# Up projection of an encoder's MLP as seven block products, with weight sums that grow in one buffer

## The chip, the cores and the metric

One core of one Trainium2 chip runs the whole kernel. The metric is the device time of one execution in microseconds; the time of a kernel is the median of several runs.

## The reference

One encoder layer on 512 tokens of width 1024 in float32: a mixer of two recurrent head groups, cross-attention on 256 memory tokens, and an MLP, each behind an RMSNorm and added to the residual stream, with one more RMSNorm at the end. The change lies in the MLP and in the passage to it.

```python
def squared_relu_mlp(xn, w_up, w_down):
    return jnp.square(jax.nn.relu(xn @ w_up)) @ w_down

x = x + cross_attention(rmsnorm(x, norm_xattn), rmsnorm(mem, norm_mem), w_xq, w_xkv, w_xo)
x = x + squared_relu_mlp(rmsnorm(x, norm_mlp), w_up, w_down)
return rmsnorm(x, norm_final)
```

w_up is 1024 x 4096, w_down 4096 x 1024.

## The kernel before

**Products.** Every float32 operand is split in two parts, hi (a rounded copy, made by ACT) and lo (the rest, made by DVE); `split_out` (L257, L258) issues both. A product takes three matmuls: hi hi, hi lo, lo hi (`mm3`, L261 to L263, and L1153 to L1155 in the block products). Weights arrive in blocks of 128x1024 (512 KB).

**The MLP** goes through the 4096 inner columns in four groups f of 1024. Each f has an up stage, then a down stage. Up is computed with the weights stationary and the 512 tokens as the moving columns: `proj_d` (L274 on) takes 8 blocks of 128 inner columns, each 8 k tiles of `mm3` on 128x512, 192 matmuls for an f. Result blocks leave PSUM through one DVE instruction that applies relu and 1/rms of the token (L1342, the row `rrow` is made by `rms_row`, L1264), and ACT squares them (L1343). DVE and ACT then form sums and differences of token and inner-column halves, and their hi and lo parts (L1349 to L1366), as operands of down.

**Down** and the attention's output projection before it ("xo") already run as seven block products (`by_blocks`, L1135 on): tokens, inner columns and output columns are halved, P1 to P7 are products of sums of token/inner blocks with sums of weight blocks (Winograd's form of Strassen's scheme), and each product is added with a sign to one or two result blocks (`INTO`). Each product comes in two parts g, so that a stage has 14 jobs of 12 matmuls of 128x512 (168 for a down stage). P1, P2 and P3 use plain weight blocks. The sums for P4 to P7 are made by DMA: GpSimd's queue loads a block and then adds others into it with accumulating DMAs (`add_block` L1100, L1102; `sum_loads` L1086). A sum that has been split for one product is added to once more, and serves another (for down, the buffer of P6 becomes that of P4).

**Order.** PE's order is the program's. A job's weights are split up to three jobs ahead (`ahead`), and loaded by SyncE's queue (`load`, L232 on) three blocks ahead of that; `st`, `wh` and `wl` have three buffers each. Weight sums lie in two buffers of 2 x 1024 ("as") and four of 1024 ("gate"). DVE, ACT, GpSimd and SyncE work in the order in which the instructions stand in their queues.

**The passage into up.** The last product of xo is P4. As x (`vv`) is completed block by block, `turn_two` (L1230) transposes 128x128 pieces on PE, eight at a time, and ACT and DVE make hi and lo of x times the norm's gain (L1242, L1243). x is not divided by its rms here. `first_two` (L1305) computes up's first two blocks in halves of k, so that the last x blocks are transposed in between.

Of the kernel before, what the change touches and what calls it, by code (L numbers as in the profile page):

```python
# [45 lines left out]
def _split_order():  # L46
# [30 lines left out]
NSTREAM = len(SEQ) - 10  # L77
# [3 lines left out]
def trunk(ctx: ExitStack, tc: tile.TileContext, x, mem, wpk, vec, cst, lmask, rmask, rows, out):  # L81
# [994 lines left out]
    ORDER = ("P1", "P2", "P6", "P5", "P7", "P3", "P4")  # L1076
    LATE = [(p, g) for p in ORDER[2:] for g in range(2)]
    JOBS = {f: [("P1", 0), ("P2", 0), ("P1", 1), ("P2", 1)] + LATE for f in range(4)}

    JOBS[-1] = [(p, g) for p in ("P1", "P7", "P2", "P5", "P6", "P3", "P4") for g in range(2)]  # L1080
# [5 lines left out]
    def sum_loads(f, names):  # L1086

        parts = {"T2": ((0, 1), (1, 1), (0, 0)), "U": ((0, 1), (0, 0)), "T3": ((0, 1), (1, 1))}
        for nme in names:
            if nme == "T3":  # L1090
                t2 = [G4()[:, :] for _ in range(2)]
            else:
                t = A16()
                t2 = [t[:, g * 1024:g * 1024 + 1024] for g in range(2)]
            for g in range(2):
                sums[f, nme, g] = t2[g]
        return [add_block(sums[f, nme, g], block(f, g, *parts[nme][i]), i > 0)
                for i in range(3) for nme in names for g in range(2) if i < len(parts[nme])]
# [6 lines left out]
    SUMS = {f: {"P6": "T2", "P5": "U", "P7": "T3", "P4": "T2"} for f in range(4)}  # L1105
    SUMS[-1] = {"P6": "T3", "P5": "U", "P7": "T3", "P4": "T3"}

    def job(f, n):

        if n >= len(JOBS[f]):  # L1110
            if f < 3:
                split(SIDX["d", "up", 0, 1024 * (f + 1)] + n - len(JOBS[f]))
            return None
        p, g = JOBS[f][n]
        if p in PLAIN:
            i = block(f, g, *PLAIN[p])
            split(i)
            return hl_tiles[i]
        if (f, n) not in jobs_hl:
            s_ = sums[f, SUMS[f][p], g]  # L1120
            hi, lo = T("wh", 1024, 3, F32R), T("wl", 1024, 3, F32R)
            made = split_out(hi, lo, s_)
            if f < 0 and n == 2:
                for a, b in zip(made, q_made[0]):
                    behind(a, b)
            jobs_hl[f, n] = (hi, lo)
            if f < 0 and p == "P7":
                add_block(s_, block(f, g, 0, 0))
            if p == "P6":
                add_block(s_, block(f, g, 1, 0))  # L1130
        return jobs_hl[f, n]
# [4 lines left out]
    INTO = {f: INTO for f in range(4)}  # L1136
    INTO[-1] = {**INTO[0], "P6": [(2, 1, -1), (0, 1, -1)], "P7": [(2, 1, -1), (2, 0, 1)]}
    LAST = {f: {("P2", 0, 0), ("P3", 0, 1), ("P4", 2, 0), ("P7" if f >= 0 else "P6", 2, 1)} for f in JOBS}

    def by_blocks(f, sta, banks, done, ready=None, after=None):  # L1140

        user = {"P1": 0, "P2": 1, "P5": 2, "P6": 0, "P3": 2, "P7": 0 if f >= 0 else 3, "P4": 0}
        opens = {"P1", "P2", "P5"} if f >= 0 else {"P1", "P2", "P5", "P7"}
# [15 lines left out]
        def ahead(n):  # L1159
            with tc.high_priority():  # L1160
                for m in range(n, n + 3):
                    job(f, m)
# [3 lines left out]
            if n == 8 and 0 <= f < 3:  # L1166
                sum_loads(f + 1, ("U", "T3"))
            return job(f, n)

        def finished(p, u):  # L1170
            for t0, c, sign in INTO[f][p]:
                done(t0 + u, c, held[user[p]][u], sign, (p, t0, c) in LAST[f])

        n = 0
        while n < len(JOBS[f]):
# [287 lines left out]
```

## Time and profile before

| | |
|---|---|
| median of 3 runs | 832.43 us (832.4 to 832.55) |
| profiled execution | 832.41 us, span 830.3 us |
| granted TensorE clock | 0.998 |
| PE, PEld, DVE, ACT busy | 99%, 82%, 72%, 52% of the span |
| GpSimd busy (with its DMA issues) | 77.4 us, 9% |
| DMA moved | 118.86 MB: 77.80 by hardware queue q1 (SyncE's), 39.85 by software queue q0 (GpSimd's) |
| last product of xo begins, up begins | 488.60 us, 494.94 us |

A row of a timeline is: start, duration, engine, line, operation, output <- inputs, shape, and in brackets the idle time of the engine before it and what ended it. PE is TensorE, PEld its weight loads, POOL GpSimd; an "x8" folds eight of the same. A matmul's duration reaches from its issue to the end of its result, so neighbours overlap; distances between starts say what one takes of PE. A row of the DMA queues has packets, MB and the share of the 16 DMA engines' time. A row of the DMA issues has the count, the size and the median time from issue to landing.

### The profile page before, as it was taken

The numbers are of one execution on the slowest core, as the hardware profiler recorded it, in microseconds if no ns is written. First come the engines' busy times: TensorE is split into PE (matmuls) and PEld (weight loads), VectorE is DVE, ScalarE is ACT, GpSimd is POOL, SyncE is SP. The second block draws the span as 40 slices with busy tenths as digits, with TensorE's granted clock in tenths as the row PEclk, the third lists the DMA queues.
The fourth block names the chain that finished last, engine by engine and source line by source line (L and its number), as shares of the span: only waits on it lengthen the run. The fifth ranks groups of instructions, "written<-read, shape, count | busy, mean of one in ns | idle before, by whom it ended". The sixth has DMA issues, their size and how long they took to land.

```text
span 830.3 us, 11722 instructions
## 1 busy us (share of the span) xinstructions
PE 818.2 (99%) x4414; PEld 681.7 (82%) x4414; DVE 594.5 (72%) x1046; ACT 430.0 (52%) x767; POOL 77.4 (9%) x131
## 2 busy tenths in 40 slices
PE   8999999999999999999999999999999999999996
PEld 6788888887878989887888888888888888888885
DVE  6568875699569988555558985676568666756685
ACT  5247455443678475455546575453444345434544
POOL 2000000100010000100000004012102210220001
PEclk9999999999999999999999999999999999999999
DMA  7332223222342344532352349969836982798332
GB/s 276 117 133 78 77 78 102 79 89 79 117 123 68 123 138 147 151 98 85 118 127 60 84 124 299 264 158 270 238 102 176 274 214 98 185 293 206 109 69 102
DMA packets 34122, 118.86 MB, mean 143 GB/s; under 512 B 3921, under 2 KB 4049, under 8 KB 34066
## 3 DMA queue, kind: packets, MB, share of 16 engines
q1 hardware_dynamic: 22832, 77.80, 27.4%
q0 software_dynamic: 10944, 39.85, 21.7%
q8 instruction: 35, 0.57, 0.3%
q10 hardware_dynamic: 290, 0.47, 0.2%
q14 instruction: 21, 0.17, 0.1%
HBM read 116.00 MB, written 2.10 MB: 142 GB/s over the span
## 4 chain that ended last, share of the span: by engine, by line
PE 89%; issue 5%; DVE 2%; DMA 1%; ACT 1%; POOL 1%; POOLq 0%; ACTq 0%
PE mm L261 18%; PE mm L263 18%; PE mm L262 18%; PE sm L1155 6%; PE sm L1153 6%; PE sm L1154 6%; PE sm L485 2%; PE mm L1155 2%; PE mm L1153 2%; PE mm L1154 2%; PE sm L827 1%; PE sm L562 1%; DVE wl L258 1%; PE sm L263 1%; PE sm L261 1%
## 5 line engine op out<-in xcount | busy, mean ns | idle before, releaser
L258 ACT ACTIVATE wh<-st 128x1024 fp32r<-128x1024 f32 x131 | 138.7, 1060 | 189.8 <-PE mm L262 117.8
L261 PE MATMUL mm<-xT,wh 128*128 128x512 f32 x544 | 215.2, 396 | 0.0
L258 DVE TENSOR_TENSOR wl<-st,wh 128x1024 fp32r<-128x1024 f32 x131 | 160.2, 1224 | 75.5 <-ACT wh L258 75.0
L263 PE MATMUL mm<-xT,wl 128*128 128x512 f32 x544 | 213.0, 392 | 0.1
L262 PE MATMUL mm<-xT,wh 128*128 128x512 f32 x544 | 212.3, 390 | 0.3 <-DVE xT L975 0.3
L263 PEld LDWEIGHTS mm<-xT,wl 128*128 128x128 f32 x544 | 102.1, 188 | 21.7 <-DVE wl L258 0.3
L262 PEld LDWEIGHTS mm<-xT,wh 128*128 128x128 f32 x544 | 102.2, 188 | 21.0 <-DVE xT L975 0.9
L261 PEld LDWEIGHTS mm<-xT,wh 128*128 128x128 f32 x544 | 102.2, 188 | 20.9 <-ACT wh L258 0.3
L1102 POOL DMA_DIRECT2D as<-in_wpk x52 | 39.6, 764 | 250.2 <-DVE wl L258 165.1
L1342 DVE SCALAR_TENSOR_TENSOR t<-mm,rg 128x512 f32<-128x512 f32 x32 | 22.0, 691 | 52.1 <-PE mm L263 52.0
L1153 PE MATMUL sm<-wh,yT 128*128 128x512 f32 x128 | 49.8, 389 | 0.0
L1154 PE MATMUL sm<-wl,yT 128*128 128x512 f32 x128 | 49.8, 389 | 0.0
L1155 PE MATMUL sm<-wh,yT 128*128 128x512 f32 x128 | 49.8, 389 | 0.0
L258 ACT ACTIVATE wh<-as 128x1024 fp32r<-128x1024 f32 x26 | 27.6, 1062 | 37.0 <-PE sm L1155 23.7
L258 DVE TENSOR_TENSOR wl<-as,wh 128x1024 fp32r<-128x1024 f32 x26 | 31.9, 1226 | 14.0 <-ACT wh L258 13.9
L1153 PE MATMUL sm<-wh,a 128*128 128x512 f32 x84 | 32.9, 391 | 0.0
L1155 PE MATMUL sm<-wh,a 128*128 128x512 f32 x84 | 32.7, 389 | 0.0
L1154 PE MATMUL sm<-wl,a 128*128 128x512 f32 x84 | 32.7, 389 | 0.0
L1285 DVE TENSOR_TENSOR vv<-vv,sm 128x512 f32<-128x512 f32 x48 | 31.0, 681 | 1.7 <-PE sm L1155 1.7
L199 POOL TENSOR_TENSOR tiny<-tiny,misc 128x4 f32<-128x4 f32 (+1 forms) x10 | 9.6, 963 | 204.6 <-DVE tiny L197 139.5
L1154 PEld LDWEIGHTS sm<-wl,yT 128*128 128x128 f32 x128 | 24.0, 188 | 5.0
L1155 PEld LDWEIGHTS sm<-wh,yT 128*128 128x128 f32 x128 | 24.0, 188 | 5.0
(329 smaller groups left out, 1581.1 us busy)
## 6 DMA issues: line engine op xcount, KB each, us to landing
st<-in_wpk SPq DMA_DIRECT2D x131, 512.0 KB, 3.4
as<-in_wpk POOLq DMA_DIRECT2D x52, 512.0 KB, 7.0
gate<-in_wpk POOLq DMA_DIRECT2D x24, 512.0 KB, 6.9
as<-in_x SPq DMA_DIRECT2D x4, 512.0 KB, 6.7
vv<-in_x SPq DMA_DIRECT2D x8, 256.0 KB, 4.5
out<-vv SPq DMA_DIRECT2D x7, 256.0 KB, 2.2
a<-in_mem SPq DMA_DIRECT2D x2, 512.0 KB, 3.7
t<-in_rows SPq DMA_DIRECT2D x2, 256.0 KB, 4.9
```

The lines of the kernel that those rows point to most:

```text
L199: gp.tensor_tensor(out=r, in0=ms, in1=nh.to_broadcast([P, w]), op=ALU.pow)
L258: return sc.activation(dst_hi, src, AF.Copy), v.tensor_tensor(out=dst_lo, in0=src, in1=dst_hi.bitcast(F32), op=ALU.subtract)
L261: pe.matmul(ps, lhsT=ah, rhs=bh, start=first, stop=False)
L262: pe.matmul(ps, lhsT=ah, rhs=bl, start=False, stop=False)
L263: pe.matmul(ps, lhsT=al, rhs=bh, start=False, stop=last)
L485: mm = pe.matmul(ps[64 * i:64 * i + 64, z:z + 64], lhsT=kc[j][:, w * P + 64 * i:w * P + 64 * i + 64], rhs=rhs(j, w * P, i), start=True, st ...
L1102: return gp.dma_start(out=dst, in_=wpk[idx], **kw)
L1153: pe.matmul(ps, lhsT=ah, rhs=bh, start=new, stop=False, **fl)
L1154: pe.matmul(ps, lhsT=ah, rhs=bl, start=False, stop=False, **fl)
L1155: pe.matmul(ps, lhsT=al, rhs=bh, start=False, stop=end and k == 1, **fl)
L1285: added = v.tensor_tensor(out=z, in0=z, in1=ps, op=ALU.add if sign > 0 else ALU.subtract)
L1342: v.scalar_tensor_tensor(out=y, in0=ps, scalar=0.0, in1=rrow[:, 0:512], op0=ALU.max, op1=ALU.mult)
```

## The change

Up becomes seven block products too, and up and down share one list of jobs for the MLP's eight stages (st = 0 to 7; even ones are up).

- Up: an f has 14 jobs (`MORDER`) of 24 matmuls of 128x256 (256 tokens), 336 for an f (L1468 to L1470). Its blocks are halves of tokens, of inner columns and of the 1024 inputs. Results stay in PSUM over several products (bank A of P1 grows by P6, P7 and P4) and are copied or added from there by ACT and DVE; relu and square are two ACT instructions.
- x is multiplied by 1/rms before the products. `rstd_half` gets 1/rms for each token half (GpSimd's power, L1348), `norm_half` spreads it over rows (two transposes and an ACT copy), `times_r` (L1355) multiplies x blocks of 128x512, and DVE and ACT form the seven operands and their hi and lo parts once, for all four f. `flip` does the transposes; `later` and `after_product` put them between matmuls.
- Weight sums, up and down alike: the P5 sum is split, added to for P6, split, added to for P4, all in one buffer (`chain_buf`); P7 has another (`pair_buf`). The two "as" buffers swap these parts from stage to stage. The "gate" buffers no longer hold weight sums in the MLP. A stage has 8 accumulating and 4 plain DMAs on GpSimd's queue and 6 plain ones on SyncE's. Before, an up and a down stage together had 10 accumulating and 6 plain on GpSimd's and 14 on SyncE's. Up's blocks are read from DRAM in rows of 2 KB (`128x2x512`).
- The order of products in down is now P1, P2, P5, P3, P6, P7, P4 (P6, P5, P7, P3, P4 behind P1 and P2 before). Up's first sums are issued from job 8 of xo on.

```diff
-        for j in range(4):
-            seq += d("up", 1024 * f + P * j, 1) + d("up", 1024 * f + P * (j + 4), 1)
+        for g in range(2):
+            seq += d("up", 1024 * f + 256 * g, 2) + d("up", 1024 * f + 512 + 256 * g, 2)
...
+    MORDER = [("P1", 0), ("P2", 0), ("P1", 1), ("P2", 1)] + [(p, g) for p in ("P5", "P3", "P6", "P7", "P4") for g in range(2)]
+    MJ = [(st, p, g) for st in range(8) for p, g in MORDER]
...
+    def mblock(st, g, kh, c):
+        f = st // 2
+        if st % 2:
+            return wpk[block(f, g, kh, c)]
+        i = SIDX["d", "up", 0, 1024 * f + 512 * c + 256 * g]
+        return wpk[i:i + 2, :, kh * 512:kh * 512 + 512].rearrange("n p c -> p n c")
...
+    def chain_buf(st, g):
+        return msum[st % 2][:, g * 1024:g * 1024 + 1024]
+
+    def pair_buf(st, g):
+        return chain_buf(st + 1, g)
+
+    def sum_start(st, pair):
+        if st < 8:
+            for i, b in enumerate(((0, 1), (1, 1) if pair else (0, 0))):
+                for g in range(2):
+                    mfill(gp, (pair_buf if pair else chain_buf)(st, g), st, g, b, i > 0)
...
+    def msplit(n):
...
+            src = mst[n][:, :] if p in PLAIN else (pair_buf if p == "P7" else chain_buf)(st, g)
+            hi, lo = T("wh", 1024, 3, F32R), T("wl", 1024, 3, F32R)
+            split_out(hi, lo, src)
...
+            if p == "P5":
+                adds.append(mfill(gp, src, st, g, (1, 1), True))
+            if p == "P6":
+                mfill(gp, src, st, g, (1, 0), True)
+            if g == 1 and p in ("P7", "P4"):
+                sum_start(st + 1, p == "P4")
...
+    def mahead(n):
+        with tc.high_priority():
+            for m in range(n, n + 3):
+                msplit(m)
+            for m in range(n + 3, n + 7):
+                mload(m)
+        return mhl[n]
...
+            if n == 8:
+                msum.extend([A16(), A16()])
+                sum_start(0, False)
+                sum_start(0, True)
...
     def add_out(t, c, ps, sign, last):
...
+        if (t, c) == (2, 0):
+            turn_x2[0] = [smb(), smb()]
+            later.append([1, lambda: flip(turn_x2[0], (2,), 0)])
+        elif (t, c) == (3, 0):
+            later.append([0, lambda: flip(turn_x2[0], (3,), 0)])
+            later.append([1, lambda: norm_half(1)])
...
+    def times_r(x, u, h):
+        z = x[:, h * 512:h * 512 + 512]
+        r = rrow[:, u * 256:u * 256 + 256]
+        v.tensor_tensor(out=z.rearrange("p (k t) -> p k t", t=256), in0=z.rearrange("p (k t) -> p k t", t=256),
+                        in1=r.unsqueeze(1).to_broadcast([P, 2, 256]), op=ALU.mult)
...
+    def norm_half(u):
+        ps = smb()
+        for t in range(2):
+            pe.transpose(ps[:, t * P:t * P + P], rt[u][:, t:t + 1].to_broadcast([P, P]), ident)
+        with tc.high_priority():
+            sc.activation(rrow[:, u * 256:u * 256 + 256], ps[:, 0:256], AF.Copy)
+            for p, x in ((("P1", fx[0, 0]), ("P2", fx[0, 1])) if u == 0 else (("P5", sraw[0]),)):
+                for h in range(2):
+                    times_r(x, u, h)
+                    part_split(p, x, h)
...
+    def up(st):
...
+        for n, (p, g) in enumerate(MORDER):
+            hi, lo = mahead(len(MORDER) * st + n)
...
+            ps = B[g] if p == "P2" else C[g] if p in ("P5", "P3") else A[g]
+            xh, xl = xf[p]
+            for k in range(2):
+                o = ps[:, k * 256:k * 256 + 256]
+                for kt in range(4):
+                    z = slice(k * 512 + kt * P, k * 512 + kt * P + P)
+                    m = slice(kt * 256, kt * 256 + 256)
+                    new = k == kt == 0 and p in ("P1", "P2", "P5")
+                    pe.matmul(o, lhsT=hi[:, z], rhs=xh[:, m], start=new, stop=False, **fl)
+                    pe.matmul(o, lhsT=hi[:, z], rhs=xl[:, m], start=False, stop=False, **fl)
+                    pe.matmul(o, lhsT=lo[:, z], rhs=xh[:, m], start=False, stop=kt == 3, **fl)
+                after_product()
...
     for f in range(4):
...
-                y = T2()[:, 0:512]
-                v.scalar_tensor_tensor(out=y, in0=ps, scalar=0.0, in1=rrow[:, 0:512], op0=ALU.max, op1=ALU.mult)
-                sc.activation(y, y, AF.Square)
...
+        sta = up(2 * f)
...
+        by_blocks(2 * f + 1, sta, (sm2, mm2, mm2), lambda t, c, ps, sign, last: add_to(t, c, ps, sign, f == 3 and last))
```

Two places in the order. The first is DVE at the end of xo. `vv_530` and `vv_531` are the last two blocks of x that P4 completes; `xT` are operands of up, `wl` lo parts of weights, `a4` x blocks, `rg` the row of 1/rms. Before, from one of these additions to the other:

```order
L1222 TENSOR_TENSOR vv_530_3315<-vv_530_3315,mm_694_4302 128x512
L1243 SCALAR_TENSOR_TENSOR xT_693_4299<-sm_767_4705,vc_68,xT_693_4299 128x256 x2
L1243 SCALAR_TENSOR_TENSOR xT_693_4299<-sm_768_4714,vc_68,xT_693_4299 128x256
L258 TENSOR_TENSOR wl_765_4688<-st_745_4567,wh_764_4687 128x1024
L1243 SCALAR_TENSOR_TENSOR xT_693_4299<-sm_768_4714,vc_68,xT_693_4299 128x256
L1222 TENSOR_TENSOR vv_531_3317<-vv_531_3317,mm_695_4303 128x512
```

After:

```order
L1299 TENSOR_TENSOR vv_530_3315<-vv_530_3315,mm_701_4309 128x512
L1355 TENSOR_TENSOR a4_751_4577<-a4_751_4577,rg_700_4308 128x512 x2
L1355 TENSOR_TENSOR a4_782_4724<-a4_782_4724,rg_700_4308 128x512
L258 TENSOR_TENSOR xT_692_4298<-a4_751_4577,xT_692_4298 128x512
L258 TENSOR_TENSOR wl_779_4705<-st_759_4615,wh_778_4704 128x1024
L258 TENSOR_TENSOR wl_792_4782<-st_764_4641,wh_791_4781 128x1024
L258 TENSOR_TENSOR xT_692_4298<-a4_751_4577,xT_692_4298 128x512
L258 TENSOR_TENSOR xT_692_4298<-a4_782_4724,xT_692_4298 128x512
L1355 TENSOR_TENSOR a4_782_4724<-a4_782_4724,rg_700_4308 128x512
L1299 TENSOR_TENSOR vv_531_3317<-vv_531_3317,mm_702_4310 128x512
```

Four transposed parts of x (L1243) and one weight split stood between the two additions; now four multiplications by 1/rms, three splits of up's operands and two weight splits do.

The second is GpSimd's queue there. `gate` are the weight sums of xo (the rows of gate_630 and gate_631 at L1096 are L1102 before), `as` the buffers of the MLP's sums, the row that makes `tiny` from `tiny` and `misc` is the power for 1/rms. Before:

```order
L1102 DMA gate_630_3958<-in_wpk 128x1024 [waits DMASW1_49,DVE_49]
L1102 DMA gate_631_3959<-in_wpk 128x1024 [waits DMASW3_49,DVE_49]
L1102 DMA gate_630_3958<-in_wpk 128x1024 [waits DMASW0_49,DVE_49]
L1102 DMA gate_631_3959<-in_wpk 128x1024 [waits DMASW1_49,DVE_49]
L1261 TENSOR_TENSOR tiny_773_4745<-tiny_772_4743,misc_73 128x4 [waits DVE_49,Pool_49]
L1102 DMA as_775_4748<-in_wpk 128x1024 [waits DMAHW7_49,DMAHW6_49,PE_49]
L1102 DMA as_775_4748<-in_wpk 128x1024
L1102 DMA as_776_4749<-in_wpk 128x1024 [waits DMASW7_49,DMASW6_49]
L1102 DMA as_776_4749<-in_wpk 128x1024
```

After:

```order
L1141 DMA as_755_4589<-in_wpk 128x2x512 [waits DMAHW6_49,DMAHW7_49,DVE_49,PE_49]
L1141 DMA as_755_4589<-in_wpk 128x2x512
L1141 DMA as_755_4589<-in_wpk 128x2x512 [waits DMASW2_49]
L1141 DMA as_755_4589<-in_wpk 128x2x512 [waits DMASW3_49]
L1141 DMA as_756_4590<-in_wpk 128x2x512 [waits DMASW7_49,DMASW6_49,DVE_49]
L1096 DMA gate_630_3958<-in_wpk 128x1024 [waits DMASW0_49,DVE_49]
L1141 DMA as_756_4590<-in_wpk 128x2x512
L1141 DMA as_756_4590<-in_wpk 128x2x512 [waits DMASW6_49,DMASW1_49]
L1096 DMA gate_631_3959<-in_wpk 128x1024 [waits DVE_49]
L1141 DMA as_756_4590<-in_wpk 128x2x512 [waits DMASW0_49]
```

The last additions to gate_630 and gate_631 stood alone, ahead of the power and of the MLP's sums; now transfers of up's sums stand before them, between them and behind them, all eight ahead of the power.

More of the change, by code (lines that the diff above doesn't have):

```diff
@@ L1218, in heads_in, with after_product @@
             drain()
+    later = []
+    def after_product():
+        for w in list(later):
+            w[0] -= 1
+            if w[0] < 0:
+                later.remove(w)
+                w[1]()
+    fx, rt, sraw = {}, {}, [None]
     def add_out(t, c, ps, sign, last):
         z = xr[t, c]
[L1222 to L1223 removed]
+        v.tensor_tensor(out=z, in0=z, in1=ps, op=ALU.add if sign > 0 else ALU.subtract)
+        if not last:
+            return
+        with (tc.high_priority() if (t, c) in ((1, 1), (3, 0)) else ExitStack()):
```

317 lines of the change are left out of this document (176 added, 141 removed).

## The prediction

> **What bounds the kernel now.** I read the page first: the busy shares, then the chain that ended last.
>
> ```profile
> span 830.3 us, 11722 instructions
> PE 818.2 (99%) x4414; PEld 681.7 (82%) x4414; DVE 594.5 (72%) x1046; ACT 430.0 (52%) x767; POOL 77.4 (9%) x131
> PE 89%; issue 5%; DVE 2%; DMA 1%; ACT 1%; POOL 1%; POOLq 0%; ACTq 0%
> ```
>
> TensorE is busy for 99% of the span and carries 89% of the chain. The list of PE's waits has eight rows, of which these are the two longest; all the lines named in it lie in earlier stages than the MLP.
>
> ```profile
> PE sm L601 <- DVE t L594: 1.1, 2, 0.6
> PE sm L349 <- DMA cs<-in_cst: 1.0, 1, 1.0
> ```
>
> So from the up projection to the last matmul no wait is to be gained. Time can come only from fewer or cheaper PE instructions, and can be lost only where another engine now arrives late. The windows show what the others carry there (us, PE, PEld, DVE, ACT, POOL, granted clock, DMA share, GB/s; an up stage, the down stage that follows, and the next two):
>
> ```profile
> 588.00:632.00 44.00, 44.00 (x196) 36.44 (x195) 32.17 (x50) 22.92 (x32) 2.57 (x3) 1.00 0.50 141
> 632.00:670.00 38.00, 38.00 (x170) 31.45 (x169) 23.02 (x27) 13.69 (x14) 9.83 (x14) 1.00 0.97 255
> 670.00:714.00 44.00, 44.00 (x196) 36.44 (x195) 32.56 (x51) 22.93 (x32) 2.11 (x3) 1.00 0.50 140
> 714.00:752.00 38.00, 38.00 (x170) 31.45 (x169) 22.62 (x26) 13.72 (x15) 9.43 (x13) 1.00 0.96 251
> ```
>
> Up leaves the DMA engines half idle; down keeps them at 0.97 and PE still doesn't wait. An f pair (up and down) has 44 + 38 us of PE work and 0.50 x 44 + 0.97 x 38 = 58.9 us of DMA work.
>
> **PE's own work: the gain.** Up has 768 matmuls of 128x512 before (4 f x 8 blocks x 8 k x 3) and 1344 of 128x256 after (4 f x 14 jobs x 24). The duration of a row is the matmul's latency; what counts is the distance between starts. PE's timeline has both widths in unbroken runs, 12 steps from the first row to the second, and 24 from the third to the fourth:
>
> ```profile
> 470.42 0.39 PE L1153 MATMUL sm<-wh,a 128*128 128x512 f32 x1
> 473.14 0.39 PE L1153 MATMUL sm<-wh,xT 128*128 128x512 f32 x1
> ...
> 397.58 0.28 PE L261 MATMUL sm<-a,yT 128*128 128x256 f32 x1
> 400.45 0.40 PE L261 MATMUL mm<-xT,wh 128*128 128x512 f32 x1
> ```
>
> A full one is 2.72 / 12 = 0.2267 us, a half one 2.87 / 24 = 0.1196 us, 0.53 of it. Up goes from 768 x 0.2267 = 174.1 us to 1344 x 0.1196 = 160.7 us: **-13.4 us**. It would break even at 174.1 / 1344 = 0.1295 us. Each matmul has its own weight load, which in the same half-width stretch is longer than that distance and yet holds nothing up:
>
> ```profile
> L263 PEld LDWEIGHTS sm<-a,yT 128*128 128x128 f32 x8 | 1.5, 192 | 0.0
> ```
>
> The Trainium skill, page TensorE: Matmul & The Clock Gate, section Back-to-back issue gap, speaks against the change: sustained about 131 ns per matmul at 512 columns and 81 at 128, hence on a line about 98 at 256; by that up would go from 100.6 to 131.7 us and the kernel would be 31 us slower. The section's isolated gap, N/2.4 + 2.5 ns, would give 165.7 and 146.8 us instead, a gain of 18.9. The trace agrees with neither (226.7 and 119.6 ns), and the sum goes by the trace.
>
> **DVE and ACT inside up: nothing.** After, an up stage has on DVE 14 weight splits (lo) and 28 operations on 128x512, on ACT 14 weight splits (hi) and 36 on 128x512. Their distances in busy stretches:
>
> ```profile
> 540.90 1.23 DVE L258 TENSOR_TENSOR wl<-st,wh 128x1024 fp32r<-128x1024 f32 x1 [0.17 <-ACT wh L258]
> 542.04 0.42 DVE L1358 TENSOR_TENSOR t<-t,t 128x256 f32<-128x256 f32 x1
> 542.38 0.68 DVE L258 TENSOR_TENSOR a<-t,a 128x512 fp32r<-128x512 f32 x1
> 542.98 0.42 DVE L1359 TENSOR_TENSOR t<-t,t 128x256 f32<-128x256 f32 x1
> ```
>
> ```profile
> 539.81 1.06 ACT L258 ACTIVATE wh<-st 128x1024 fp32r<-128x1024 f32 x1 [3.40 <-PE mm L262]
> 540.77 0.62 ACT L1343 ACTIVATE t<-t 128x512 f32<-128x512 f32 x1
> 543.72 1.14 ACT L258 ACTIVATE yT<-t 128x512 fp32r<-128x512 f32 x2
> ```
>
> DVE: 14 x 1.14 + 28 x 0.60 = 32.8 us. ACT: 14 x 0.96 + 36 x 0.57 = 34.0 us. PE has 336 x 0.1196 = 40.2 us in that time, so both are covered (82 and 85%). A job is 24 x 0.1196 = 2.87 us and weights are split up to three jobs ahead, so a late result of one job has one job's time before PE sees it. Bounds: 0, and one job's 2.87 us once per stage if the order turns out badly; I take 0, since down before has the same three jobs of lead and no wait.
>
> **The DMA engines.** A pair has 20 plain and 10 accumulating transfers of 512 KB before, 20 and 16 after. What one takes of the sixteen engines, in a stretch of 10 us with two accumulating ones alone, in one of 15 us with plain ones alone, and in a full one (552 to 590 us):
>
> ```profile
> q0 software_dynamic: 288, 1.05, 65.3%
> ...
> q1 hardware_dynamic: 334, 1.23, 27.0%
> ...
> q0 software_dynamic: 1920, 6.96, 77.2%
> q1 hardware_dynamic: 771, 2.83, 19.0%
> ```
>
> Alone: 6.53 / 2 = 3.27 us accumulating, 4.05 us for 2.35 transfers = 1.72 plain. In the full stretch: 7.2 us for 5.4 plain = 1.34, and 29.3 us for 13.3 of GpSimd's, which at its 10 to 6 ratio are 8.3 accumulating and 5 plain: (29.3 - 5 x 1.34) / 8.3 = 2.72. After, a pair needs between 16 x 2.72 + 20 x 1.34 = 70.3 us and 16 x 3.27 + 20 x 1.72 = 86.7 us, against PE's 40.2 + 38.1 = 78.3. The same prices make 54.0 and 67.1 of before's measured 58.9; scaled by that, both ends come to 76 us, 97%. Tight, but down before ran 38 us at 0.97 without a wait.
>
> ```profile
> 473.52 0.86 POOL L1102 DMA_DIRECT2D gate<-in_wpk  x1 [19.58 <-DVE wl L258]
> 476.87 0.85 POOL L1102 DMA_DIRECT2D gate<-in_wpk  x1 [2.49 <-DVE wl L258]
> ...
> as<-in_wpk POOLq DMA_DIRECT2D x9, 512.0 KB, 7.0
> ...
> gate<-in_wpk POOLq DMA_DIRECT2D x4, 512.0 KB, 8.5
> ```
>
> What can be late is the second half of a chain, in which P5's split, an accumulating transfer into the same buffer, and P6's split follow each other. P6 is four jobs behind P5, 11.5 us less the split's two steps (0.96 + 1.14) and 0.86 us of issue: 8.5 us, and up to a job more, since weights are split ahead. The landings of the same full stretch (7.0 and 8.5 us) just fit. I take **+1 us** in all, with 0 and 29 us (below) as ends.
>
> **The passage from the attention output into up: the loss.** Before, the scale by 1/rms is applied to up's results, so PE starts up on half of x unscaled, and the last transposes sit 2.72 us behind the end of the attention output (494.94 us) without a wait (PE's timeline, with DVE's between):
>
> ```profile
> 486.35 1.04 PE L1236 MATMUL sm<-cs,vv 128*128 128x128 f32 x8
> 487.14 0.48 PE L1153 MATMUL sm<-wh,a 128*128 128x512 f32 x1
> ...
> 488.60 0.39 PE L1153 MATMUL mm<-wh,yT 128*128 128x512 f32 x1
> ...
> 494.94 1.23 DVE L258 TENSOR_TENSOR wl<-st,wh 128x1024 fp32r<-128x1024 f32 x1 [0.44 <-ACT wh L258]
> 496.08 0.48 DVE L1243 SCALAR_TENSOR_TENSOR xT<-sm,vc,xT 128x256 fp32r<-128x256 f32 x1
> 496.47 0.68 DVE L1222 TENSOR_TENSOR vv<-vv,mm 128x512 f32<-128x512 f32 x1
> ...
> 497.66 1.03 PE L1236 MATMUL sm<-cs,vv 128*128 128x128 f32 x8
> ```
>
> After, P1's x block must be scaled before its first matmul, and the order on DVE puts the last addition to x (buffer 531) behind that work. On PE, from the start of P4 of the attention output (488.60, t = 0): 8 transposes, 6 matmuls, 8 transposes, 6 matmuls (4.3 us, with 487.14 - 486.35 = 0.79 for 8 transposes and 0.2267 a matmul), the two transposes of the first half's 1/rms, 12 matmuls, 4 transposes of buffer 530, the first half of P1, 4 transposes of buffer 531, the second half of P1, the second half's 1/rms, P2. With 0.5 us for 4 transposes, 0.35 for 2 (half and a quarter of 0.79, and an estimated 0.1 for the change of form) and 1.44 for half a job, P2 would start at about 11.7 without waits. On DVE, once 1/rms lies there (copied by ACT at about 5.3): four multiplications, three splits of x and the addition to buffer 530, at 0.60 each, and two weight splits at 1.14 come ahead of the addition to 531: 4.8 + 2.3 = 7.1 us, then 0.7 for itself, so that it ends at about 13.1. PE's second part of P1's first half needs the x split behind both weight splits and gets it at about 10.7 (5.3 + 5 x 0.60 + 2 x 1.14); it reaches the transposes of 531 at 11.9, waits 1.25 us for it, and after P1 waits 0.65 us more for DVE's statistics and GpSimd's power. P2 starts at 16.0: 4.3 us of waiting, to which comes 1.0 us at P3, whose x split stands behind P5's forms, the sums of L1377 to L1383 and five weight splits. **+5.3 us**; ends 1 (DVE idle enough to run ahead of my replay) and 8 (ACT's splits late as well). Split transposes add 0.15 us.
>
> ```profile
> 498.72 1.03 POOL L1261 TENSOR_TENSOR tiny<-tiny,misc 128x4 f32<-128x4 f32 x1 [21.00 <-DVE tiny L981]
> 499.72 2.19 POOL L1102 DMA_DIRECT2D as<-in_wpk  x4
> ```
>
> GpSimd's queue also changes: the first eight transfers of up's sums now stand among the two additions for P4's weights and ahead of the power. Before, those additions went out at 473.52 and 476.87 (rows above) with the queue empty, and the sums only from 499.72. After, the second addition is behind seven of the eight, one of which waits for another to land. P4's second weights are first used at 488.6 + 0.8 + 1.4 + 0.8 = 491.6, so their split must begin by 489.4. If the buffers are free early, the addition still goes out near 477 and lands 8.5 us later, at 485.5: 0. If the queue is full, five transfers of 2.72 to 3.27 us stand before its landing, 490.6 to 493.4: up to 4 us. The first is nearer to the row of before; I take **+1.5**.
>
> **Sum**, against the profiled execution's 832.41 us (2.1 us more than its span, which stay; the median of the runs is 832.43): 832.4 - 13.4 + 0.15 + 5.3 + 1.5 + 1.0 = **827.0 us**. What follows the last matmul is not touched.
>
> **Rivals.**
> The DMA engines become the bound (slower). Place: P6's weight split behind P5's addition; it decides once an accumulating transfer costs over (78.3 - 20 x 1.34) / 16 = 3.2 us. At the price of one alone, 86.7 - 78.3 = 8.4 us a pair in three and a half pairs is 29 us: 827 + 29 = 856; with half of that, 841. For: 97% by the calibrated sum, 16 additions that come in twos. Against: full stretches show 2.72. In the Trainium skill, page DMA: Bandwidth & Descriptors, section Issuing engines are not separate DMA queues, transfers of all issuing engines share the same sixteen; the two shares of the full stretch (77.2 and 19.0%) bear that out. Chance 0.23.
> The passage eats the gain: 8 us on DVE and 4 on GpSimd's queue, 832.4 - 13.3 + 12 = 831.1, no change. Chance 0.10.
> The passage is hidden: 1 us, and nothing at GpSimd: 832.4 - 13.3 + 1 = 820.1. My replay is of an order, not of a trace, so 0.10.
> Half-width matmuls lose their cover: weight loads of 0.192 us no longer lie under neighbours, 1344 x 0.192 = 258 us, 84 slower (911). The row of 24 at 0.1196 speaks against it; the rule above goes the same way. Chance 0.02.
>
> **How the numbers follow.** The forecast has 0.55. A measurement can tell 0.2%, 1.7 us. Faster: 0.55 + 0.10 = 0.65; same 0.10; slower 0.23 + 0.02 = 0.25. The range goes from the hidden passage, 820, into the DMA rival to 846, five us past its half, which leaves out some 0.15. The cases that are faster have 820 to 830.7.
>
> **What would show it.** In the profile after: 24 matmuls of up in 2.87 us; PE waits of 4 to 6 us in all between 488 and 510, on DVE's splits and on buffer 531; none later over 1 us; DMA shares of 0.9 and more in up as in down. It is wrong if PE waits in every pair for splits that wait for a transfer, if half-width matmuls stand further apart than 0.1295 us, or if the passage has no wait.

## The result and the profile after

The changed kernel takes 871.31 us (median of 4 runs, 871.24 to 872.54) against 832.45 us beside it: 1.047 times as long, 95% interval 1.0452 to 1.0488. The forecast was 827.0 us, with a range up to 846.

The page after. PE's busy time is 3 us more, although up's matmuls take 12.8 us less (below), because matmuls at a lower clock are shown longer. PE's share falls from 99 to 94% and the granted clock to 0.978 of full speed; DVE, ACT and DMA appear in the chain. GpSimd's DMA queue goes from 39.85 to 56.63 MB.

```profile
span 869.5 us, 13071 instructions
PE 821.4 (94%) x4990; PEld 706.6 (81%) x4990; DVE 624.2 (72%) x1033; ACT 482.1 (55%) x850; POOL 116.4 (13%) x164
...
q0 software_dynamic: 19648, 56.63, 31.6%
...
PE 66%; DVE 12%; issue 7%; DMA 7%; ACT 6%; POOL 1%; POOLq 0%; ACTq 0%; DVEq 0%
```

PE's waits now have four long rows (total, times, longest), where before none lay in this part of the program. Lines L1211 are the block products of the attention output and of down, L1415 is DVE's addition of a product to the residual stream in down, L1299 the same in the attention output, L1325 the transposes of x. L1425 belongs to the statistics of the final norm, which in the last down stage stand among DVE's additions.

```profile
PE mm L1211 <- DVE vv L1415: 18.3, 3, 7.0
PE sm L1325 <- DVE vv L1299: 6.3, 2, 5.8
PE mm L1211 <- DVE tiny L1425: 5.6, 1, 5.6
PE sm L1211 <- DVE vv L1415: 3.4, 8, 0.7
```

By stage, taken from the first matmul of each on PE's timeline:

| stage | before, us | after, us | difference |
|---|---|---|---|
| attention output's P4 and transposes, up to up's first matmul | 6.34 | 15.12 | +8.8 |
| up, f = 0 | 44.89 | 46.33 | +1.4 |
| up, f = 1, 2, 3 | 43.52 each | 40.31, 40.31, 40.32 | -9.6 |
| down, f = 0, 1, 2, 3 | 38.08, 38.08, 38.08, 38.09 | 46.55, 47.56, 48.67, 48.16 | +38.6 |

The sum is +39.2 us, the difference of the spans. Up does what was forecast. The loss lies in down, whose matmuls are the same in number and shape as before, and in the passage.

The windows of up and down for f = 1 and f = 2 (the same columns as in the prediction, here cut at the stages' first matmuls). Up is without a gap and keeps the DMA engines at 0.98; down, with 40.9 us of PE busy in 47.6 or 48.7, has them at 0.8 and a granted clock of 0.93.

```profile
596.60:636.91 40.31, 40.31 (x338) 40.31 (x337) 25.88 (x28) 27.85 (x40) 11.34 (x13) 1.00 0.98 238
636.91:684.47 47.56, 40.95 (x171) 32.83 (x169) 33.59 (x44) 20.36 (x25) 10.82 (x13) 0.93 0.83 198
684.47:724.78 40.31, 40.31 (x337) 40.31 (x336) 25.96 (x28) 27.96 (x40) 10.09 (x12) 1.00 0.99 235
724.78:773.45 48.67, 40.92 (x170) 32.76 (x169) 33.59 (x44) 20.13 (x25) 10.71 (x13) 0.93 0.81 195
```

Inside down, PE's timeline at the place of the longest waits (f = 0), where P5 ends and P3 begins:

```profile
566.17 0.39 PE L1213 MATMUL mm<-wh,a 128*128 128x512 f32 x1
572.02 0.77 PE L1211 MATMUL mm<-wh,a 128*128 128x512 f32 x1 [5.46 <-DVE vv L1415]
572.59 0.63 PE L1212 MATMUL mm<-wl,a 128*128 128x512 f32 x1
573.01 0.63 PE L1213 MATMUL mm<-wh,a 128*128 128x512 f32 x1
...
575.08 0.39 PE L1212 MATMUL mm<-wl,a 128*128 128x512 f32 x1
575.30 0.39 PE L1213 MATMUL mm<-wh,a 128*128 128x512 f32 x1
```

P3 uses the PSUM bank that P5 has just filled, so PE waits for DVE to add P5's result to the residual stream. Six matmuls behind the wait stand 0.43 us apart, twice the usual distance; the granted clock in that stretch is half:

```profile
566.17:572.02 5.85, 0.39 (x2) 0.03 (x1) 5.85 (x9) 1.06 (x1) 0.85 (x1) 0.96 0.65 193
572.02:574.50 2.48, 2.48 (x6) 2.02 (x7) 0.46 (x1) 0.00 (x0) 0.00 (x0) 0.50 1.06 195
```

And DVE at the same time. It is not waiting; it works without a gap, and the additions (L1415) stand behind the work that was queued ahead:

```profile
562.38 0.69 DVE L1415 TENSOR_TENSOR vv<-vv,sm 128x512 f32<-128x512 f32 x1
562.98 1.23 DVE L258 TENSOR_TENSOR wl<-st,wh 128x1024 fp32r<-128x1024 f32 x1
564.12 0.69 DVE L258 TENSOR_TENSOR a<-rg,a 128x512 fp32r<-128x512 f32 x1
564.72 0.69 DVE L258 TENSOR_TENSOR a<-t,a 128x512 fp32r<-128x512 f32 x1
565.32 0.69 DVE L258 TENSOR_TENSOR a<-as,a 128x512 fp32r<-128x512 f32 x1
565.92 1.23 DVE L258 TENSOR_TENSOR wl<-st,wh 128x1024 fp32r<-128x1024 f32 x1
567.05 0.69 DVE L258 TENSOR_TENSOR a<-t,a 128x512 fp32r<-128x512 f32 x1
567.66 0.69 DVE L258 TENSOR_TENSOR a<-as,a 128x512 fp32r<-128x512 f32 x1
568.26 1.23 DVE L258 TENSOR_TENSOR wl<-as,wh 128x1024 fp32r<-128x1024 f32 x1
569.39 0.69 DVE L1415 TENSOR_TENSOR vv<-vv,sm 128x512 f32<-128x512 f32 x1
569.99 2.48 DVE L1415 TENSOR_TENSOR vv<-vv,mm 128x512 f32<-128x512 f32 x4
```

The `a` rows are lo parts of operand forms for P3, P6 and P7 (g = 0 and 1). Before, the forms were made column block by column block while up was still running; now they are sums of whole halves, most of which need up's last two products, P7 and P4, and the program issues all of them ahead of down's first addition (only P1's first, at 562.38, has come between them in DVE's queue). The four additions of 569.99 are P2's two, then P5's two. The third of them, which frees the first half of P3's bank, ends at about 571.9, and PE goes on at 572.02; P5's matmuls had ended at 566.56.

At the same place before (down f = 0 begins at 539.83) P1's two additions start 7.9 us and P2's 10.6 us into the stage:

```profile
547.71 1.28 DVE L1285 TENSOR_TENSOR vv<-vv,sm 128x512 f32<-128x512 f32 x2
550.43 1.28 DVE L1285 TENSOR_TENSOR vv<-vv,mm 128x512 f32<-128x512 f32 x2
```

In the changed kernel (from 550.05) it is 12.3 and 19.3 us for P1's two and 19.9 us for P2's.

### The profile page after: what moved, and what is told of

It is laid out like the page before. It is cut to its first block, busy times and chain, and to the rows that moved or that the text cites. A ratio compares the mean times of both kernels' runs of the same rounds, so it can differ in the third digit from the quotient of the medians.

```text
span 869.5 us, 13071 instructions
## 1 busy us (share of the span) xinstructions
PE 821.4 (94%) x4990; PEld 706.6 (81%) x4990; DVE 624.2 (72%) x1033; ACT 482.1 (55%) x850; POOL 116.4 (13%) x164
## 3 DMA queue, kind: packets, MB, share of 16 engines
q0 software_dynamic: 19648, 56.63, 31.6%
## 4 chain that ended last, share of the span: by engine, by line
PE 66%; DVE 12%; issue 7%; DMA 7%; ACT 6%; POOL 1%; POOLq 0%; ACTq 0%; DVEq 0%
PE mm L261 11%; PE mm L263 11%; PE mm L262 11%; DVE wl L258 5%; ACT wh L258 4%; DMA st<-in_wpk 3%; PE mm L1469 3%; PE mm L1470 3%; PE mm L1468 3%; PE sm L485 2%; PE sm L1211 2%; PE sm L1213 2%; PE sm L1212 2%; DVE a L258 2%; DVE vv L1415 2%
## 5 line engine op out<-in xcount | busy, mean ns | idle before, releaser
L258 DVE TENSOR_TENSOR wl<-as,wh 128x1024 fp32r<-128x1024 f32 x66 | 80.8, 1225 | 61.3 <-ACT wh L258 61.0
L1141 POOL DMA_DIRECT2D as<-in_wpk x96 | 86.9, 920 | 280.0 <-DVE wl L258 163.0
L258 ACT ACTIVATE wh<-as 128x1024 fp32r<-128x1024 f32 x66 | 69.7, 1056 | 92.9 <-PE mm L1213 35.1
L261 PE MATMUL mm<-xT,wh 128*128 128x512 f32 x288 | 115.4, 402 | 0.0
L263 PE MATMUL mm<-xT,wl 128*128 128x512 f32 x288 | 113.4, 394 | 0.1
L262 PE MATMUL mm<-xT,wh 128*128 128x512 f32 x288 | 112.8, 392 | 0.2 <-DVE xT L975 0.2
L263 PEld LDWEIGHTS mm<-xT,wl 128*128 128x128 f32 x288 | 54.1, 188 | 11.7 <-DVE wl L258 0.3
L262 PEld LDWEIGHTS mm<-xT,wh 128*128 128x128 f32 x288 | 54.2, 188 | 11.0 <-DVE xT L975 0.9
L261 PEld LDWEIGHTS mm<-xT,wh 128*128 128x128 f32 x288 | 54.2, 188 | 11.0 <-ACT wh L258 0.3
L1211 PE MATMUL mm<-wh,a 128*128 128x512 f32 x68 | 30.5, 449 | 23.9 <-DVE vv L1415 18.3
L1211 PE MATMUL sm<-wh,a 128*128 128x512 f32 x116 | 45.9, 395 | 3.4 <-DVE vv L1415 3.4
L1211 PEld LDWEIGHTS mm<-wh,a 128*128 128x128 f32 x68 | 14.9, 219 | 28.6 <-issue 19.5
L1469 PE MATMUL sm<-xT,wh 128*128 128x256 f32 x128 | 36.7, 287 | 1.0 <-DVE xT L258 1.0
L1468 PE MATMUL sm<-xT,wh 128*128 128x256 f32 x128 | 36.9, 288 | 0.6 <-ACT xT L258 0.6
L1470 PE MATMUL sm<-xT,wl 128*128 128x256 f32 x128 | 36.6, 286 | 0.0
L1468 PE MATMUL mm<-xT,wh 128*128 128x256 f32 x128 | 36.3, 284 | 0.0
L1468 PE MATMUL sm<-yT,wh 128*128 128x256 f32 x128 | 36.2, 283 | 0.0
```

The source lines that it names most:

```text
L258: return sc.activation(dst_hi, src, AF.Copy), v.tensor_tensor(out=dst_lo, in0=src, in1=dst_hi.bitcast(F32), op=ALU.subtract)
L261: pe.matmul(ps, lhsT=ah, rhs=bh, start=first, stop=False)
L262: pe.matmul(ps, lhsT=ah, rhs=bl, start=False, stop=False)
L263: pe.matmul(ps, lhsT=al, rhs=bh, start=False, stop=last)
L1141: return eng.dma_start(out=dst, in_=mblock(st, g, *b), **kw)
L1211: pe.matmul(ps, lhsT=ah, rhs=bh, start=new, stop=False, **fl)
```

## The experiments

The main theory after this profile: **DVE's in-order queue**. A burst of forms at the start of down stands ahead of the additions that empty PSUM, and the new order of products needs a bank again before the burst is through. Its two parts were tried one by one: the order of the banks (e1) and the place in the queue (e2), later the forms themselves (e13). The rival is the prediction's own: **the DMA engines** are the bound and everything behind them is late (e3). The passage was looked at by itself (e4). All times stand against 871.3 us after and 832.3 to 832.6 us before. e1 to e4, e7 and e13 are one execution each; of the kernels with several, the changed one scatters by 1.3 us and e12, the widest, by 8.

**e1, the order of the banks.**

```diff
+    DORDER = [(p, g) for p in ("P1", "P5", "P2", "P6", "P3", "P7", "P4") for g in range(2)]
-    MJ = [(st, p, g) for st in range(8) for p, g in MORDER]
+    MJ = [(st, p, g) for st in range(8) for p, g in (DORDER if st % 2 else MORDER)]
...
-        jobs = MORDER if mlp else JOBS
+        jobs = DORDER if mlp else JOBS
...
-    LAST = {True: {("P2", 0, 0), ("P6", 0, 1),
+    LAST = {True: {("P2", 0, 0), ("P3", 0, 1),
```

> Against 871.3 us of the changed kernel. Only the order of down's products changes, to P1, P5, P2, P6, P3, P7, P4, so that no product but P4 follows one in the same PSUM bank. Theory 1 (PE waits for DVE to empty the bank that the product before it filled): in each of four down stages the wait of 5.5 to 7 us between P5 and P3, the slow matmuls behind it (about 1.5 us) and the shorter one between P6 and P7 (about 0.8 us) go: some 8 x 4 = 32 us, 836 to 842 us, down stages of 38.5 to 40 us. Theory 2 (the DMA engines are the bound, and splits come late): the transfers are the same, 866 to 875 us.

870.05 us: nothing gained, and theory 1 as put there has fallen. PE's waits show why:

```profile
PE sm L1212 <- DVE vv L1416: 22.4, 7, 8.0
```

The wait has moved to P6, which writes P1's bank (in the first down stage 2.8 us more there are for P6's own form). Two products, P5 and P2, lie between P1 and P6, but P1's additions stood behind the same forms. So it isn't the neighbourhood of two products in one bank that costs; any bank that is needed again within DVE's burst is late. That the time stayed doesn't speak for the DMA theory either, as the wait is still one for DVE's additions.

**e2, the place in the queue.**

```diff
-        added = v.tensor_tensor(out=z, in0=z, in1=ps, op=ALU.add if sign > 0 else ALU.subtract)
+        with tc.high_priority():
+            added = v.tensor_tensor(out=z, in0=z, in1=ps, op=ALU.add if sign > 0 else ALU.subtract)
```

> Against 871.3 us. The order of products stays; DVE's additions to the residual stream in down get priority over the forms in DVE's queue. Theory 1a (same bank, and DVE's queue of late forms makes the wait long): the wait at P3 shrinks from 6 us to 0.5 to 1.5 us, the two short ones stay: 843 to 850 us. Theory 1b (the same bank alone makes the wait, whatever stands in the queue): 868 to 873 us. Theory 2 (DMA): 866 to 875 us.

846.82 us, 24.5 us less, by the order of DVE's queue alone. Theory 1a holds. PE's waits:

```profile
PE sm L1325 <- DVE vv L1299: 6.7, 2, 5.8
PE mm L1211 <- DVE vv L1416: 3.2, 3, 1.6
PE sm L1211 <- DVE vv L1416: 2.7, 7, 0.4
```

The wait at the transposes of the passage is as it was; those at P3 are down from 18.3 and 5.6 us to 3.2 and one of 0.8 us for ACT. Down's four stages take 28 us less; up's first two take 1.8 us more each, so that 24.5 are left.

**e3, the accumulating transfers.**

```diff
-        kw = dict(accum_op=ALU.add) if accumulate else {}
+        kw = {}
         if st % 2 == 0:
```

> Against 871.3 us. All 64 accumulating transfers of the MLP write plainly in place of adding, so the weight sums are left out (each buffer holds its last block), with the same count, sizes, queues and waits. Theory 1: at most the passage into up gains, 862 to 872 us, and the waits at P3 in down stay at 5 to 7 us. Theory 2: 64 x (2.7 to 3.3 less 1.3 to 1.7) = 64 to 128 us of engine time less, and the waits go: 835 to 848 us.

867.01 us. All weight sums are replaced by plain copies and the waits at P3 are still there:

```profile
PE mm L1211 <- DVE vv L1415: 16.3, 3, 6.0
PE mm L1211 <- DVE tiny L1425: 5.0, 1, 5.0
PE sm L1325 <- DVE vv L1299: 4.7, 2, 3.8
```

Of the 4.3 us gained, 2 are the wait at the transposes (5.8 to 3.8). The DMA engines did become less busy, from 0.98 to 0.74 in up and from 0.83 to 0.59 in down (f = 1):

```profile
594.40:634.71 40.31, 40.31 (x337) 40.31 (x336) 26.05 (x28) 27.95 (x40) 7.63 (x13) 1.00 0.74 242
634.71:682.06 47.35, 41.57 (x171) 33.22 (x169) 33.50 (x44) 20.70 (x25) 7.62 (x12) 0.93 0.59 195
```

Down's stage is 0.2 us shorter for it (47.35 for 47.56). The DMA engines are not what costs the 39 us.

**e4, GpSimd's queue in the passage.**

```diff
-                add_block(s_, block(-1, g, 1, 0))
+                q_made.append(add_block(s_, block(-1, g, 1, 0)))
...
-                    mfill(gp, (pair_buf if pair else chain_buf)(st, g), st, g, b, i > 0)
+                    m = mfill(gp, (pair_buf if pair else chain_buf)(st, g), st, g, b, i > 0)
+                    if st == 0 and pair:
+                        behind(m, q_made[-1])
```

> Against 871.3 us. The four transfers that start up's second pair of sums stand behind both additions for xo's P4 in GpSimd's queue, and the rest is as changed. If the late addition (issued at 482.74 us, landed about 493) makes the stall at xo's P4, PE's wait of 5.85 us at the transposes and the slow matmuls behind it go: 862 to 865 us, and the addition is issued by 477 us. If the landing is late because the DMA engines are full, the wait shrinks by less than 3 us: 868 to 872 us.

865.60 us, 5.7 us less, 0.6 above the upper end of the range. What it undoes is seen in the changed kernel's GpSimd rows, where the queue stands until a transfer has landed, with the second addition for the attention output behind it:

```profile
474.21 1.11 POOL L1141 DMA_DIRECT2D as<-in_wpk  x1
482.01 1.20 POOL L1141 DMA_DIRECT2D as<-in_wpk  x1 [6.68 <-DMA as<-in_wpk]
482.74 1.36 POOL L1096 DMA_DIRECT2D gate<-in_wpk  x1
```

ACT, which splits that block, then waits for it until 493.10:

```profile
493.10 1.06 ACT L258 ACTIVATE wh<-gate 128x1024 fp32r<-128x1024 f32 x1 [6.46 <-DMA gate<-in_wpk]
```

DVE, in its order, makes the lo part of that block first, and only then the additions to x for which PE's transposes wait, until 496.07:

```profile
494.19 1.23 DVE L258 TENSOR_TENSOR wl<-gate,wh 128x1024 fp32r<-128x1024 f32 x1 [6.92 <-ACT wh L258]
495.33 1.28 DVE L1299 TENSOR_TENSOR vv<-vv,sm 128x512 f32<-128x512 f32 x2
```

With the edit both additions go out as they did before, at 473.57 and 476.92, and the wait moves to transfers that nobody needs yet:

```profile
473.57 0.87 POOL L1096 DMA_DIRECT2D gate<-in_wpk  x1 [0.69 <-DVE wl L258]
476.92 0.84 POOL L1096 DMA_DIRECT2D gate<-in_wpk  x1 [2.48 <-DVE wl L258]
477.46 1.76 POOL L1141 DMA_DIRECT2D as<-in_wpk  x2
488.09 1.23 POOL L1141 DMA_DIRECT2D as<-in_wpk  x1 [8.86 <-DMA as<-in_wpk]
```

The wait of 5.85 us at the transposes is gone, so the queue's order made it. The speed of the transfers has a part in its length: in e3, with the queue as changed and plain transfers, 3.8 us of it stay.

**e13, the forms themselves.** Down's P3, P6 and P7 use P5's operands:

```diff
-        for g in range(2):
-            v.tensor_tensor(out=y[3, g], in0=y[3, g], in1=y[0, g], op=ALU.subtract)
...
-            form("P7", g, y[0, g], A4)
+        for g in range(2):
+            for p in ("P3", "P6", "P7"):
+                forms[p, g] = forms["P5", g]
```

> Against 871.3 us, with nothing else changed. The operands of P3, P6 and P7 of down are not formed: P5's stand in for them, so those three products are computed from wrong operands. That takes 12 operations of 128x512 from DVE (7.2 us) and 6 from ACT at the start of each down stage. If these forms, ahead of the additions in DVE's queue, make PE's wait at P3, it shrinks from 5.5 to 7 us to under 1.5 us although no addition was given priority: 841 to 848 us. If the weight splits and transfers make it, 866 to 872 us.

843.28 us, 28.0 us less, with the order of products and every transfer as changed and no addition moved by hand. PE's waits:

```profile
PE sm L1325 <- DVE vv L1299: 6.5, 2, 5.8
PE sm L1211 <- DVE vv L1415: 3.4, 8, 0.8
PE mm L1211 <- DVE vv L1415: 1.6, 4, 0.4
```

P3 now waits 0.4 us in each of the four stages, like P7 and P4 (0.8 us at the last P4). Down's stages take 40.1 us (40.5 the last), some 30 us less in all; up's first stage takes 1.7 us more. This and e2 reach the same place from two sides: fewer forms ahead of the additions, or the additions ahead of the forms.

**e7, e2 and e4 together.**

> The changed kernel with both single edits that helped: down's additions first in DVE's queue (846.8 us alone) and up's second pair of sums behind the additions for xo's P4 in GpSimd's queue (5.7 us less alone). The two waits lie 60 us apart, so if they have separate causes the gains add: 840 to 842 us. If the earlier passage only moves the wait into the next stage, 844 to 847 us.

835.12 us: 36.2 us less, where the sum of the two is 30.2. In e4 up begins 7.9 us earlier than in the changed kernel, and 2.2 us of that are given back, 1.0 in up's first stage and the rest in down; in e2 the second up stage has two short waits (0.8 and 0.2 us) and the first down stage one for ACT (0.8 us). In this run these waits are gone. But e12, the same kernel in seven executions, goes from 835.0 to 843.4 us (27.9 to 36.3 less), and its profile, of the slowest, has the two waits in up again: that the gains more than add is not shown. Up's later stages are 40.31 us here, down's 39.9 to 41.1.

**e5 and e8, with e1's order of products in addition, and with the last addition to x earlier.** The edit of e8 beyond e5:

```diff
-        v.tensor_tensor(out=z, in0=z, in1=ps, op=ALU.add if sign > 0 else ALU.subtract)
+        with (tc.high_priority() if last and (t, c) == (3, 0) else ExitStack()):
+            v.tensor_tensor(out=z, in0=z, in1=ps, op=ALU.add if sign > 0 else ALU.subtract)
```

> The same with down's products in the order P1, P5, P2, P6, P3, P7, P4, which did nothing alone (870.05 us). If the order of the PSUM banks matters once DVE's additions are early, the waits of 0.7 to 1.8 us at P3 and of 0.4 us at P7 go and one of 0.4 us per down stage stays: some 1.5 us per stage, 833 to 837 us. If the bank order has no part in it, 839 to 842 us. If P5's forms are late in their new place (second product of down), PE waits there for ACT or DVE and the time is over 842 us.

> The kernel with all three edits, and the last addition to x (buffer 531, the one that the prediction followed) ahead of two weight splits in DVE's queue. If PE's waits behind P4 of xo are ended by that addition, 1 to 2.5 us less than with the three; if they are ended by the scaled and split halves of P1's x block, the same within 0.7 us.

867.91 us (864.51 to 870.66) and 868.68 us (864.93 to 869.17); e5 stands at 1.042 of before, interval 1.0397 to 1.0443. I had expected 833 to 837. The waits of e5:

```profile
PE sm L1214 <- ACT a L258: 18.3, 4, 5.1
PE sm L1216 <- DVE a L258: 11.5, 4, 3.1
```

This time PE waits not for additions but for an operand form. The order P1, P5, P2, P6 uses P6's form two jobs earlier than before, while DVE and ACT still make P3's ahead of it; and the additions now take their turns ahead of both. e8 says nothing new: in its passage the wait for buffer 531 (0.5 us) is gone and that for P1's second half is 1.9 us in place of 1.0.

**e9 and e10, forms in the order in which the products use them.** e9 makes P6's form ahead of P3's; e10 also has e8's earlier addition and moves the passage's two weight splits behind P1's x block. The edit of e9 beyond e5:

```diff
             v.tensor_tensor(out=y[3, g], in0=y[3, g], in1=y[0, g], op=ALU.subtract)
+            form("P6", g, y[3, g], A4)
+        for g in range(2):
             v.tensor_tensor(out=y[1, g], in0=y[1, g], in1=y[3, g], op=ALU.add)
             form("P3", g, y[1, g], A4)
-        for g in range(2):
-            form("P6", g, y[3, g], A4)
```

> The three edits that gave 867.9 us, with P6's form made ahead of P3's in DVE's and ACT's queues, as down's new order of products uses them. If PE's waits of 4 to 5 us and 3 us per down stage in that kernel came from P6's form standing behind P3's (and not from the bank order or the transfers), they go, and the bank order saves the 0.6 to 2 us per stage that are left with the old order (835.1 us): 829 to 833 us. If the new order of products itself is harmful (sums of weights too late for P5 as second product), still over 840 us, with waits for splits of weights.

> The same, and in the passage into up both halves of P1's x block and the last addition to x stand ahead of the weight splits for P2 and for the second part of P1. PE's waits between P4 of xo and P2 of up (3.7 us with the two earlier edits) should shrink to under 1.5 us if those splits' place in DVE's and ACT's queues makes them: 2 to 3 us less than the run beside it. If 1/rms itself comes too late, the same within 0.7 us.

e9: 846.50 us (ratio 1.0167, interval 1.0149 to 1.0185). 21 us of e5's loss was the order of the forms, so that part of the theory holds, but the order of products stays 10 us worse than the other. ACT's waits for transfers in e9:

```profile
ACT wh L258 <- DMA as<-in_wpk: 32.9, 13, 5.6
ACT wh L258 <- DMA st<-in_wpk: 9.1, 2, 4.9
```

Here the rival's mechanism does appear: the sums come too late for ACT, 13 times, and PE waits 5.7 us for weight splits, beside 4.3 us for forms. In the changed kernel, from 520 us on, ACT waits 14.2 us in all for plain blocks and never for a sum. Which of the moved steps does it (P5 two jobs earlier, or the chain of P5, P6 and P4 spread otherwise) was not tried. e10, 854.90 us (1.0269, 1.0254 to 1.0284), took P1's wait away (1.6 to 0.2 us) and got waits of 3.2 us at the second half's 1/rms, 1.8 us at P2 and 3.7 us at P3 in exchange: a miss.

**e11 and e12.** e11 is e7 with only those additions first whose bank the next product uses; e12 is e7 once more, in seven executions.

```diff
-        with tc.high_priority():
+        with (tc.high_priority() if c and (t > 1 or sign < 0) else ExitStack()):
```

> The two edits that gave 835.1 us, but in DVE's queue only those additions of down go first whose PSUM bank the next product uses again (of P5, P6 and P7); those of P1 to P4 stand where they stood. If the 1 to 2 us that PE still waits at P3 come from the four additions of P1 and P2 ahead of P5's, these waits go: some 4 us in all, 830 to 832.5 us. If they come from the forms that stand ahead anyway, 834 to 836 us. If P1's additions are now late for P6, which writes P1's bank, waits of over 2 us at P6 and a time over 837 us.

> The kernel with the two edits (all of down's additions first, up's second sums behind the additions for xo's P4) once more, timed in rounds beside the kernel before: 834.5 to 836 us, 0.3% over before. If its one run of 835.1 us was a lucky order of transfers, 837 to 845 us.

e11: 837.99 us, 1.0058 (1.0045 to 1.0071); one of its six runs, of 1508.75 us, lies far from the other five, is left out of the ratio and is not explained. e12: 836.61 us, 835.01 to 843.42, 1.0064 (1.0041 to 1.0087). In e11 the waits for DVE at P3 turn into waits for ACT of 1.1 to 1.3 us, and nothing is gained; its time is over 837 us without the waits of 2 us at P6 that were to make it so. No version tried beats the kernel before; the best is 0.6% behind it. e12's runs scatter by 8 us, before's by 0.6.

## Why the prediction was wrong

**PE's own work: right.** From f = 1 on, half-width matmuls stand 0.12 us apart in up (24 from 599.47 to 602.35 us), up goes from 43.52 to 40.31 us, 3.21 x 4 = 12.8 us, forecast 13.4.

**"DVE and ACT inside up: nothing" is the step that failed**, with its last sentence: "I take 0, since down before has the same three jobs of lead and no wait." PE doesn't wait inside up from f = 1 on. But the sum put all of that work into up, and it isn't there. Of the 28 operations of 128x512 that I counted on DVE, 12 start inside up (f = 1, where DVE is busy for 25.9 of 40.3 us, 64% and not 82%) and 16 in the down stage behind it; before, 4 of 128x512 and 4 of 128x256 did. The forms made from P7 and P4 can start only when up ends, and are paid for in down. In down f = 0, 17 operations of 0.60 us and seven weight splits of 1.14 us, one per job, stand ahead of P5's additions. The three jobs of lead are for weights; the time that counts is how long a PSUM bank may wait for DVE, and with the new order of products that is shorter: P3 needs P5's bank at once, where before one or two jobs lay between two products of one bank. Down was left out of the sum as unchanged since its matmuls are. It has 38.6 of the 39.2 us, of which e13 takes some 30 away in down and e2 28; the 2.0 us a stage that e13 leaves are three short waits for the bank of the product just before.

**A wait's price was too low.** I counted a wait of one job as one job. In down f = 0, the 5.85 us from 566.17 are followed by matmuls at a granted clock of 0.50, which cost another 1.5 us; in the other three down stages the clock is 0.50 for 4.1 to 5.3 us behind the wait, and that costs 2 us and more. The waits after up begins to be fed (18.3, 5.6, 3.4, 6.3 us and three near 1 us) are 36 us, but the gaps in PE's timeline from 488 us on, against the two distances of the forecast, are 52 us. Of the other 16 us, about 13 are slow matmuls; the rest is that from start to start a wait takes some 0.2 us more than the idle time shown. The Trainium skill, page TensorE: Matmul & The Clock Gate, section What's actually happening, has the array's clock halved after an idle window of about 3.4 us until as long a busy one, and calls the window free-running. The trace agrees in the halving. Its record of the granted clock agrees with free-running windows too: in the changed kernel it changes at 506.72, 510.13, 571.57, 574.99, 656.90 and 663.73 us, always a multiple of 3.41 us apart, so how long the slow matmuls last depends on where a wait falls. It doesn't agree that a whole window must be idle: the half clock from 506.72 follows waits of only 0.6 and 1.0 us, and in e12 single waits of 1.95 and 2.17 us were followed by matmuls 0.43 us apart, while one of 1.94 us in e7 was not.

**The passage: right in kind, half in size.** Forecast 5.3 + 1.5 us. Measured: 8.8 us ahead of up, and 6.0 us by which the first up stage is longer than the others, less the 1.4 us by which it was so before: 13.4 us. With GpSimd's queue put right (e4) 6.5 of them are left, 0.9 ahead of up and 5.6 in its first stage, so some 6.9 are the queue's, against 1.5. The 6.5 are DVE's and ACT's, against 5.3, and that these are close is in part luck: the 5.3 us were waits alone, and the waits are 3.6 us in e4 and 3.0 in the changed kernel (0.6 and 1.0 us on P1's operands, 0.4 on buffer 531, 1.0 at P3); the rest is mostly slow matmuls. For 1/rms, forecast at 0.65 us, PE doesn't wait. GpSimd's queue was undersized: I took the row of before (477 us) as the likelier, and it was the full queue: the addition went out at 482.74 and landed near 493, 3.7 us beyond the 489.4 by which it was needed.

**The DMA engines: right to be close, and not the cause.** A pair takes 0.98 x 40.31 + 0.83 x 47.56 = 79 us of engine time, forecast 76. At the changed kernel's pace that is 90%, and e3 shows that making it cheaper moves little: it takes 58 us a pair there, 1.3 us less for each of 16 transfers (forecast 1.4 to 1.6), and the time is 4.3 us less. The windows from which I read up as half idle and down as 0.97 do not lie on the stages: before, up f = 1 is from 577.91 to 621.43 and down from there to 659.51, with shares of 0.66 and 0.79. The sum for a pair, 59 us, is the same, but the 38 us at 0.97 without a wait take in 10.5 us of the next up. The rival that I gave the most chance to had the right sign and the wrong mechanism. With the waits gone (e7: 0.97 in up, 0.94 in down) it becomes the next limit, as the scatter of e12 and ACT's waits in e9 suggest; that it would bind at e7's pace is argued, not shown.

**The sustained rate** that the prediction took from the Trainium skill, page TensorE: Matmul & The Clock Gate, section Back-to-back issue gap (half-width matmuls relatively dearer, 31 us slower) came near the measured loss by accident: up's matmuls as a whole did not become dearer, they take 12.8 us less.

## What to carry to other kernels

Where a stage that is "unchanged" follows a changed one on an in-order engine, replay that engine's queue through the stage: work that can only start when the first stage ends is done in the second, ahead of whatever the program issues later. For each PSUM bank ask which instruction empties it, what stands ahead of that in its queue, and which product needs the bank next; giving those few instructions priority was worth 24.5 us here. Price a long wait of PE with the slow matmuls behind it.

## What was not expected of the hardware

Behind PE waits of 5.5 to 7 us in down the granted clock was 0.50 for 2.5 to 5.3 us, 1.5 us and more on top of the wait; behind waits of 0.6 and 1.0 us close together, at the start of up, it was 0.50 from 506.7 to 510.1. In up's f = 1 stage, where part of the weight sums are read in rows of 2 KB and accumulated, the DMA engines ran at 0.98 and 238 GB/s with no wait of PE, against 255 GB/s at 0.97 in the stretch from 632 to 670 us before; with plain copies in place of the sums (e3) it was 242 GB/s at 0.74.
